# Another queue for the shift weights, earlier input transposes, and longer runs of the shift's sums

## The chip, the cores and the metric

The kernel runs on one core of one Trainium2 chip. The metric is the device time in microseconds (us). The kernel before has a median of 1969.03 us over 3 runs (1965.37 to 1971.18).

## The reference, cut to what matters

The program is one layer of an encoder over a prompt of 1024 tokens (width 2048) and 32 sample tokens, in float32. First the conditioning vector `c` of each of the two groups of tokens gives a shift, a scale and a gate by one matrix of 2048 x 6144. Then the input is normalised and modulated, and one wide projection gives the inputs of four branches:

```
shift, scale, gate = split(c @ w_mod + b_mod, 3)
u = layer_norm(x) * (1 + scale) + shift
(z_a, xbc_a, dt_a, q_b, k_b, v_b, g_b, ...) = split_cols(u @ w_in)
... four branches (state space, stick-breaking attention, mLSTM, convolution) ...
o = concat(y_a, y_b, y_c, y_d) @ w_out
x_new = layer_norm(ALPHA * x + (1 + gate) * o) * ln_g + ln_b
```

What the change touches is how `shift` and `scale` are computed at the start, and how the first `u` is made from `x`.

## The kernel before, in words

The prompt is done in two halves of 512 tokens; the 32 sample tokens ride with the first. `u` is kept transposed, as 16 tiles of 128 features by the tokens, and each tile is split into a high and a low part in a rounded float32 type (`uh`, `ul`), as are the weights (`wh`, `wl`). A product is three matmuls: `wh` by `uh`, `wh` by `ul`, `wl` by `uh` (lines 362 to 364, and 1437 to 1439 at the start). The shift is not added to `u`: it is two further columns of each tile (`shift_columns`, copied by GpSimd), so that the projection of the shift comes out of the same matmuls as two bias columns. A projection that takes those columns has to wait for the shift; one for the gates of branch B (`b_gate`, and the two gate tiles of `startup`) leaves them out and adds the bias later.

`startup` (line 1387) does what must come first. It loads and normalises the input (`load_norm`: five groups of rows, the last the 32 sample rows, four tiles of 512 columns each). It loads the scale's weights in four groups of 16 tiles of 256 KB (`quads`), and for each four tiles runs `mod_sum`: four float32 matmuls that write the four quarters of PSUM's partitions, called a quad here. When the 16 tiles of a group are summed, `mod_columns` copies the sum out of PSUM (VectorE), turns it by four transposes (TensorE), and adds and biases it into the scale of four feature tiles. Then `build_u0` makes these four feature tiles: four transposes of the input and one of the sample rows into PSUM, two scaling copies by ScalarE into `uf`, one rounding copy and one subtraction by VectorE, and a small subtraction by GpSimd. `part` multiplies four feature tiles by the weights of one gate tile, for one of two spans of tokens; four parts per group, two gate tiles by two spans. The order on TensorE and of the loads is written by hand here (`inorder`). In it, the parts of group g-1 stand between the transposes of group g.

After `startup` the rest is ordered by a planner. It simulates the program with costs of its own, puts each engine's instructions in the order in which that simulation finds them ready, and takes what the program lists first, or marks with `tc.high_priority()`, before the rest. Each engine then runs its list strictly in order. `weave` lists two more `b_gate` tiles together with the shift: `mod_group(g, 0)` for the four groups, 64 loads of 256 KB on SyncE's queue (SP), 16 quads, and four times `mod_columns`, which here ends in `shift_columns`. Then branch B's first unit follows: q, k and v of two heads, which need the shift columns.

Buffers: the pool `io` has 20 tiles, which hold the scale's and the shift's weights among others; `wk` has 13; `up` has 16 pairs for `uh` and `ul`, and 15 of the 20 input tiles are kept in it, the rest in `io`. PSUM's tags: `ip` 3 banks (accumulators of projections), `z` 2, `s` 2 and `a` 1. Nearly all loads go by SP's queue; GpSimd (POOL) issues only the stores of lines 1282 and 1340.

Of the kernel before, what the change touches and what calls it, by code (L numbers as in the profile page):

```python
# [6 lines left out]
F32 = mybir.dt.float32  # L7
# [55 lines left out]
def step_kernel(ctx, tc, xp, xs, cst, wmss, wmg, bgate, win, wsm, wout, lng, lnb, ck, cv,  # L63
# [136 lines left out]
    inorder = tc.keep_in_program_order  # L200
    begun = [None]

    def mod_sum(o, kq, ws):


        for i in (3, 0, 1, 2):
            c0 = 2 * (4 * kq + i)
            yield T.matmul(o[32 * i:32 * i + 32], cpad[:, c0:c0 + 32], ws[i][:, 0:512], start=(kq == 0),  # L208
                           stop=(kq == 3), skip_group_check=True)

    def mod_group(g, part):
        o = ZT("mod")
        for kq in range(4):
            ws = []
            for i in range(4):
                wr = IO("wmr")
                nc.sync.dma_start(wr[:, 0:512], wmss[g, 4 * kq + i, part])
                ws.append(wr)
                if i < 3:
                    yield 1  # L220
            with tc.high_priority():
                after = None
                for mm in mod_sum(o, kq, ws):
                    after = behind(mm, after)
# [26 lines left out]
    def load_norm(src, rows, keep):  # L251

        tiles = []
        for q in range(4):
            if keep and q < 3:
                t = up.tile([P, 546], F32, tag=("uh", "ul")[(len(keep) + q) % 2], name=nm("x"))
            else:
                t = (IO if keep else WK)("x")
# [12 lines left out]
        if keep:  # L271
            nb = SM(1, "bnb", 3)
            V.scalar_tensor_tensor(nb[:rows], mv[:rows, 0:1], -1.0, rs[:rows], op0=ALU.mult, op1=ALU.mult)
            for q in range(4):
                A.activation(tiles[q][:rows, 0:512], tiles[q][:rows, 0:512], AF.Identity, bias=nb[:rows],
                             scale=rs[:rows])
# [13 lines left out]
    def build_u0(xts, k):  # L290

        uh, ul = new_u(0, k)
        uf = WK("uf")
        q, o = divmod(k, 4)
        pt = ST("xt")
# [4 lines left out]
        for pp, n, c0, j in ((pt, 512, 0, 0), (pt2, SMP, 512, 1)):  # L300
            A.activation(uf[:, c0:c0 + n], pp[:, 0:n], AF.Copy, scale=scale1[:, k, j:j + 1])
        V.tensor_copy(uh[:, 2:546], uf[:, 0:544])
        return (G.tensor_tensor(ul[:, 514:546], uf[:, 512:544], uh[:, 514:546].bitcast(F32), op=ALU.subtract),
                V.tensor_tensor(ul[:, 2:514], uf[:, 0:512], uh[:, 2:514].bitcast(F32), op=ALU.subtract))
# [1081 lines left out]

    def startup():
# [27 lines left out]
        def quads(g):  # L1415
# [10 lines left out]
            for kq in range(4):  # L1426
                for mm in mod_sum(o, kq, ws[4 * kq:4 * kq + 4]):
# [18 lines left out]

        m = quads(0)
        for _ in range(3):  # L1450
            next(m)
        for g in range(4):
            o = next(m)
            m = quads(g + 1) if g < 3 else iter(())
            p = parts_of(g - 1) if g else iter(())
            next(p, None)
            mod_columns(g, 1, o, inorder)
            for i in range(4):
                if i < 3:
                    next(p, None)  # L1460
# [209 lines left out]
```

## Time and profile before

| | |
|---|---|
| Median of 3 runs | 1969.03 us |
| Profiled execution | 1967.32 us |
| Its span | 1965.3 us |
| TensorE busy | 1885.7 us, 96% |
| VectorE busy | 1343.0 us, 68% |
| ScalarE busy | 774.5 us, 39% |
| GpSimd busy | 320.5 us, 16% |
| Moved by DMA | 291.42 MB, mean 148 GB/s |

Times in the profile run from the start of the span. "Busy" is the time in which an engine had an instruction under way; matmuls overlap, so that two that start 0.127 us apart each show 0.29 us. In a row of the timeline, consecutive instructions of one kind are merged: its start, the time it takes as a whole, the engine, line, operation, tiles and shape, how many (x8), and, in brackets, how long the engine idled before it and what released it. A float32 matmul shows as two instructions, so that a quad is x8. PEclk is the clock granted to TensorE as a share of full speed.

### The profile page before, as it was taken

How to read it: one execution, taken by the hardware profiler on the slowest of the kernel's cores; microseconds unless marked ns; L12 is line 12 of the kernel's file. 1: busy time of each engine (PE TensorE's matmuls, PEld its weight loads, DVE VectorE, ACT ScalarE, POOL GpSimd, SP SyncE). 2: the span in 40 equal slices, each digit the busy share in tenths (PEclk: the TensorE clock that was granted, in tenths of full speed). 3: DMA queues.
4: the chain of work that ended last, by engine and by line, in shares of the span. 5: the costliest groups of instructions: out<-in, count | busy, mean ns of one | idle time of the engine just before them, and what ended most of it. 6: DMA issues, size and time to landing. Idle time of an engine off the chain costs nothing. (4 is left out here: it accounts for less than half of the span.)

```text
span 1965.3 us, 31995 instructions
## 1 busy us (share of the span) xinstructions
PE 1885.7 (96%) x12162; PEld 1570.6 (80%) x12162; DVE 1343.0 (68%) x2581; ACT 774.5 (39%) x1288; POOL 320.5 (16%) x542
## 2 busy tenths in 40 slices
PE   4999999999999999999999999999999899999997
PEld 1779899998888999976788786777878676778887
DVE  5416566967866858887778869885857673356665
ACT  5213433334564334545444444533335521133321
POOL 1100111211222202441101011121112320001000
PEclk9999999999999999999999999999999999999999
DMA  9885344334443343644232332432333654467643
GB/s 346 301 305 184 102 138 131 108 123 123 142 158 123 110 126 105 166 135 133 98 104 96 116 112 78 125 110 96 129 98 113 199 153 156 135 211 259 222 134 126
DMA packets 159930, 291.42 MB, mean 148 GB/s; under 512 B 23904, under 2 KB 66144, under 8 KB 159776
## 3 DMA queue, kind: packets, MB, share of 16 engines
q1 hardware_dynamic: 156960, 280.47, 44.5%
q0 software_dynamic: 2816, 8.92, 1.2%
q8 instruction: 95, 1.56, 0.3%
q14 instruction: 59, 0.48, 0.1%
HBM read 253.50 MB, written 35.82 MB: 147 GB/s over the span
## 5 line engine op out<-in xcount | busy, mean ns | idle before, releaser
L362 PE MATMUL ip<-uh,wh 128*128 128x512 f32 (+3 forms) x2304 | 759.0, 330 | 0.9 <-POOL uh L287 0.9
L364 PE MATMUL ip<-uh,wl 128*128 128x512 f32 (+3 forms) x2304 | 745.3, 323 | 0.0
L363 PE MATMUL ip<-ul,wh 128*128 128x512 f32 (+3 forms) x2304 | 745.1, 323 | 0.1
L337 ACT CAST wh<-wr 128x1024 fp32r<-128x1024 f32 x253 | 263.9, 1044 | 624.4 <-PE ip L363 343.1
L338 DVE TENSOR_TENSOR wl<-wr,wh 128x1024 fp32r<-128x1024 f32 x253 | 313.1, 1238 | 251.3 <-ACT wh L337 222.8
L362 PEld LDWEIGHTS ip<-uh,wh 128*128 128x128 f32 x2304 | 438.9, 191 | 45.2 <-issue 14.6
L364 PEld LDWEIGHTS ip<-uh,wl 128*128 128x128 f32 x2304 | 438.1, 190 | 31.7 <-issue 1.3
L363 PEld LDWEIGHTS ip<-ul,wh 128*128 128x128 f32 x2304 | 438.6, 190 | 30.9 <-issue 2.2
L1263 PE MATMUL op<-wh,yl 128*128 128x512 f32 (+1 forms) x576 | 215.2, 374 | 0.0
L1261 PE MATMUL op<-wh,yh 128*128 128x512 f32 (+1 forms) x576 | 214.9, 373 | 0.0
L1262 PE MATMUL op<-wl,yh 128*128 128x512 f32 (+1 forms) x576 | 214.4, 372 | 0.0
L1117 DVE SCALAR_TENSOR_TENSOR cv<-cin,cs,cv 128x574 f32<-128x574 f32 (+1 forms) x240 | 187.1, 780 | 2.6
L1263 PEld LDWEIGHTS op<-wh,yl 128*128 128x128 f32 x576 | 108.5, 188 | 25.6 <-issue 6.4
L1262 PEld LDWEIGHTS op<-wl,yh 128*128 128x128 f32 x576 | 108.5, 188 | 24.1 <-issue 4.8
L1261 PEld LDWEIGHTS op<-wh,yh 128*128 128x128 f32 x576 | 108.5, 188 | 22.7 <-issue 3.1
L809 POOL TENSOR_SCALAR_AFFINE_SELECT s<-s 128x128 f32<-128x128 f32 x64 | 38.3, 599 | 416.1 <-ACT s L708 415.8
L1170 DVE SCALAR_TENSOR_TENSOR gacc<-wg,cs,gacc 128x512 f32<-128x512 f32 x120 | 92.3, 789 | 11.0 <-DMA wg<-in_wmg_dram 10.9
L208 PE MATMUL mod<-wmr,cpad 128*32 128x512 f32 x256 | 38.4, 676 | 27.4 <-DMA wmr<-in_wmss_dram 27.2
L717 DVE TENSOR_TENSOR_SCAN pr<-kp 128x128 f32<-128x128 f32 (+4 forms) x66 | 53.7, 814 | 13.0 <-POOL kp L811 10.3
L721 DVE TENSOR_TENSOR s<-s,pr 128x512 f32<-128x512 f32 (+5 forms) x106 | 59.7, 566 | 1.8
L708 ACT ACTIVATE s<-z 128x512 f32<-128x512 f32 (+3 forms) x96 | 47.6, 496 | 33.1 <-PE z L738 30.5
L1071 POOL TENSOR_TENSOR dn<-dn,mhalf 128x1 f32<-128x1 f32 (+1 forms) x36 | 27.7, 770 | 194.3 <-DVE dn L1070 190.6
(384 smaller groups left out, 2342.1 us busy)
## 6 DMA issues: line engine op xcount, KB each, us to landing
wr<-in_win_dram SPq DMA_DIRECT2D x192, 512.0 KB
wmr<-in_wmss_dram SPq DMA_DIRECT2D x128, 256.0 KB
wr<-in_wout_dram SPq DMA_DIRECT2D x63, 512.0 KB
wg<-in_wmg_dram SPq DMA_DIRECT2D x64, 256.0 KB
x<-in_xp_dram SPq DMA_DIRECT2D x32, 256.0 KB
xr<-in_xp_dram SPq DMA_DIRECT2D x28, 256.0 KB
yf<-ysc SPq DMA_DIRECT2D x16, 272.0 KB
xk<-in_xp_dram SPq DMA_DIRECT2D x16, 256.0 KB
```

The costliest lines, as they stand in the source:

```text
L337: A.copy(wh, wr)
L338: V.tensor_tensor(wl, wr, wh.bitcast(F32), op=ALU.subtract)
L362: T.matmul(pt[:, 0:n], wh[:, k % 8, :], uh[:, c0:c0 + n], start=(k == 0), stop=False)
L363: T.matmul(pt[:, 0:n], wh[:, k % 8, :], ul[:, c0:c0 + n], start=False, stop=False)
L364: T.matmul(pt[:, 0:n], wl[:, k % 8, :], uh[:, c0:c0 + n], start=False, stop=(k == KD - 1))
L717: V.tensor_tensor_scan(pr[0:rows, 0:nk][:, ::-1], kp[0:rows, 0:nk][:, ::-1], kp[0:rows, 0:nk][:, ::-1], initial=init, op0=ALU.mult, op1=AL ...
L721: V.tensor_tensor(s[0:rows, 0:m], s[0:rows, 0:m], pr[0:rows, 1:m + 1], op=ALU.mult)
L1117: V.scalar_tensor_tensor(acc[:, 0:n], t[:, i:i + n], C("cdw", 31 * j + i), acc[:, 0:n], op0=ALU.mult, op1=ALU.add)
L1170: V.scalar_tensor_tensor(acc[j][:, 0:512], wr[:, 0:512], cT[:, k, j:j + 1], acc[j][:, 0:512], op0=ALU.mult, op1=ALU.add)
L1261: T.matmul(acc[t][:, 0:w], yh[:, c], wh, start=(first and i == 0), stop=False)
L1262: T.matmul(acc[t][:, 0:w], yh[:, c], wl, start=False, stop=False)
L1263: T.matmul(acc[t][:, 0:w], yl[:, c], wh, start=False, stop=(last and i == len(ws) - 1))
```

## The change

- The 64 loads of the shift's weights are issued by GpSimd on its own queue in place of SP's. During `startup` each of them is put behind one GpSimd instruction on GpSimd's list (`hold`: the small subtraction of feature tile 11).
- Twelve steps of the shift (12 loads and the first sum) are listed inside `startup`, ahead of the scale's last group.
- The shift's sums take eight weight tiles at once, as two quads in a row, in place of four. Group 0's accumulator is in PSUM tag `s`.
- `build_u0` is split. `turn_x` transposes the input of a feature tile and copies it, unscaled, from PSUM to SBUF (`xT`, mostly in free `up` tiles; ScalarE for odd tiles, VectorE for even ones). The new `build_u0` scales from SBUF: ScalarE writes `uh`, VectorE computes `x * scale - uh` in one instruction, and the 32 sample columns go by ScalarE and two GpSimd instructions.
- The transposes no longer wait for the scale. Two feature tiles are turned after each of the first three quads of group 0, and five in each of the loops of groups 0 and 1.
- The parts of group g now run in the loop of group g, between the quads of group g+1, with `mod_columns(g + 1)` ahead of the last part.
- In `load_norm`, VectorE normalises the odd ones of the four tiles, and the fourth tile is in `wk` in place of `io`.

```diff
-    def mod_sum(o, kq, ws):
+    def mod_sum(o, kq, ws, first, last):
     ...
     def mod_group(g, part):
-        o = ZT("mod")
-        for kq in range(4):
+        o = ST("mod") if g == 0 else ZT("mod")
+        for kq in range(0, 4, 2):
             ws = []
-            for i in range(4):
+            for i in range(8):
                 wr = IO("wmr")
-                nc.sync.dma_start(wr[:, 0:512], wmss[g, 4 * kq + i, part])
+                behind(nc.gpsimd.dma_start(wr[:, 0:512], wmss[g, 4 * kq + i, part]), hold[0])
                 ws.append(wr)
-                if i < 3:
+                if i < 7:
                     yield 1
             with tc.high_priority():
                 after = None
-                for mm in mod_sum(o, kq, ws):
-                    after = behind(mm, after)
+                for q in (1, 0):
+                    for mm in mod_sum(o, kq + q, ws[4 * q:4 * q + 4], kq == 0 and q == 1, kq == 2 and q == 0):
+                        after = behind(mm, after)
             yield 1
     ...
     def load_norm(src, rows, keep):
-                t = (IO if keep else WK)("x")
+                t = WK("x")
     ...
             for q in range(4):
-                A.activation(tiles[q][:rows, 0:512], tiles[q][:rows, 0:512], AF.Identity, bias=nb[:rows],
-                             scale=rs[:rows])
+                x = tiles[q][:rows, 0:512]
+                if q % 2:
+                    V.tensor_scalar(x, x, rs[:rows], nb[:rows], op0=ALU.mult, op1=ALU.add)
+                else:
+                    A.activation(x, x, AF.Identity, bias=nb[:rows], scale=rs[:rows])
     ...
-    def build_u0(xts, k):
-        uh, ul = new_u(0, k)
-        uf = WK("uf")
+    def turn_x(xts, k):
         q, o = divmod(k, 4)
+        xT = up.tile([P, 546], F32, tag=("uh", "ul")[k % 2], name=nm("xT")) if k < KD - 1 else IO("xT")
         pt = ST("xt")
         (four transposes into pt, one into pt2 = AT("xt2"), as before)
-        for pp, n, c0, j in ((pt, 512, 0, 0), (pt2, SMP, 512, 1)):
-            A.activation(uf[:, c0:c0 + n], pp[:, 0:n], AF.Copy, scale=scale1[:, k, j:j + 1])
-        V.tensor_copy(uh[:, 2:546], uf[:, 0:544])
-        return (G.tensor_tensor(ul[:, 514:546], uf[:, 512:544], uh[:, 514:546].bitcast(F32), op=ALU.subtract),
-                V.tensor_tensor(ul[:, 2:514], uf[:, 0:512], uh[:, 2:514].bitcast(F32), op=ALU.subtract))
+        if k % 2:
+            A.copy(xT[:, 0:512], pt)
+        else:
+            V.tensor_copy(xT[:, 0:512], pt)
+        V.tensor_copy(xT[:, 512:544], pt2[:, 0:SMP])
+        return xT
+
+    def build_u0(xT, k):
+        uh, ul = new_u(0, k)
+        x, h = xT[:, 0:512], uh[:, 2:514]
+        A.activation(h, x, AF.Copy, scale=scale1[:, k, 0:1])
+        x2, h2 = xT[:, 512:544], uh[:, 514:546]
+        A.activation(x2, x2, AF.Copy, scale=scale1[:, k, 1:2])
+        G.tensor_copy(h2, x2)
+        return (V.scalar_tensor_tensor(ul[:, 2:514], x, scale1[:, k, 0:1], h.bitcast(F32), op0=ALU.mult, op1=ALU.subtract),
+                G.tensor_tensor(ul[:, 514:546], x2, h2.bitcast(F32), op=ALU.subtract))
     ...
     def startup():
     ...
+        xT = []
+        def turn(n):
+            for _ in range(n):
+                xT.append(turn_x(xts, len(xT)))
         m = quads(0)
-        for _ in range(3):
-            next(m)
+        for n in (2, 2, 2, 0):
+            o = next(m)
+            turn(n)
+        mod_columns(0, 1, o, inorder)
         for g in range(4):
-            o = next(m)
+            for k in range(4 * g, 4 * g + 4):
+                begun[1:] = build_u0(xT[k], k)
+            if g == 2:
+                hold[0] = begun[2]
+                for _ in range(12):
+                    next(shift)
             m = quads(g + 1) if g < 3 else iter(())
-            p = parts_of(g - 1) if g else iter(())
-            next(p, None)
-            mod_columns(g, 1, o, inorder)
+            p = parts_of(g)
             for i in range(4):
-                if i < 3:
-                    next(p, None)
-                begun[1:] = build_u0(xts, 4 * g + i)
-                if i < 3:
-                    next(m, None)
-        for _ in parts_of(3):
-            pass
+                o = next(m, None)
+                if g < 2:
+                    turn(1)
+                if i != 2:
+                    next(p)
+            if g < 3:
+                mod_columns(g + 1, 1, o, inorder)
+            if g < 2:
+                turn(1)
+            next(p)
     ...
+    shift = chain(*[mod_group(g, 0) for g in range(4)])
     startup()
+    hold[0] = None
     ...
-            weave([(stage1(b_gate(p)), 2) for p in range(2, 4)], [(chain(*[mod_group(g, 0) for g in range(4)]), 64)])
+            weave([(stage1(b_gate(p)), 2) for p in range(2, 4)], [(shift, 52)])
```

## Rows read from the trace of the kernel before

**Rows 1.** The page, busy time by engine, and TensorE's in 40 slices.
```profile
PE 1885.7 (96%) x12162; PEld 1570.6 (80%) x12162; DVE 1343.0 (68%) x2581; ACT 774.5 (39%) x1288; POOL 320.5 (16%) x542
PE   4999999999999999999999999999999899999997
```

**Rows 2.** TensorE's waits in the span: engine, line, releaser, total us, times, longest.
```profile
PE mod L208 <- DMA wmr<-in_wmss_dram: 27.2, 11, 21.3
...
PE rt L495 <- DVE w L489: 4.4, 2, 2.5
...
PE ip L362 <- POOL uh L287: 0.9, 1, 0.9
```

**Rows 3.** Busy time by window: length, PE busy (count), PEclk, DMA share, GB/s.
```profile
21.26:94.00 72.74, 66.64 (x450) 1.00 0.94 334
94.00:155.00 61.00, 58.66 (x438) 1.00 0.87 306
```

**Rows 4.** TensorE's timeline, 21 to 39 us.
```profile
21.26 1.94 PE L208 MATMUL mod<-wmr,cpad 128*32 128x512 f32 x8 [21.26 <-DMA wmr<-in_wmss_dram]
24.16 1.94 PE L208 MATMUL mod<-wmr,cpad 128*32 128x512 f32 x8 [0.97 <-DMA wmr<-in_wmss_dram]
...
32.49 1.08 PE L233 MATMUL modc<-ident,mr 128*128 128x128 f32 x4 [0.98 <-DVE mr L231]
...
34.36 0.31 PE L299 MATMUL xt<-ident,x 32*128 32x32 f32 x1
...
36.70 1.11 PE L297 MATMUL xt<-ident,x 128*128 128x128 f32 x4
...
37.92 1.06 PE L208 MATMUL mod<-wmr,cpad 128*32 128x512 f32 x8
```

**Rows 5.** TensorE's timeline at 54.87 us, and at 93.80, the end of startup.
```profile
54.87 0.60 PE L297 MATMUL xt<-ident,x 128*128 128x128 f32 x4
55.40 0.24 PE L299 MATMUL xt<-ident,x 32*128 32x32 f32 x1
...
93.80 0.29 PE L362 MATMUL ip<-uh,wh 128*128 128x272 f32 x1
```

**Rows 6.** VectorE's and ScalarE's timelines before and after the first scale.
```profile
31.65 0.69 DVE L231 COPY mr<-mod 128x512 f32<-128x512 f32 x1 [5.96 <-PE mod L208]
33.84 0.17 DVE L240 SCALAR_TENSOR_TENSOR scale<-mods,cs 128x8 f32<-128x8 f32 x1
37.85 0.86 ACT L301 ACTIVATE uf<-xt,scale 128x512 f32<-128x512 f32 x2 [1.58 <-PE xt L297]
12.45 5.73 ACT L275 ACTIVATE x<-x,bnb,brs 128x512 f32<-128x512 f32 x8
```

**Rows 7.** VectorE on two SBUF inputs: duration ns min/median/max, first and last start.
```profile
L1170 DVE SCALAR_TENSOR_TENSOR gacc<-wg,cs,gacc x120: 655/744/1858, 456.8 to 1413.5; 128x512 f32<-128x512 f32 x120
L338 DVE TENSOR_TENSOR wl<-wr,wh x6: 1224/1224/1226, 94.1 to 141.1; 128x1024 fp32r<-128x1024 f32 x6
```

**Rows 8.** GpSimd's groups by line: count, busy us, mean ns, idle before.
```profile
L303 POOL TENSOR_TENSOR ul<-uf,uh 128x32 fp32r<-128x32 f32 x16 | 11.0, 684 | 72.4 <-DVE uh L302 72.4
```

**Rows 9.** TensorE's timeline around one quad (at 125.80) among projection matmuls.
```profile
125.58 0.29 PE L364 MATMUL ip<-uh,wl 128*128 128x272 f32 x1
...
127.03 0.28 PE L363 MATMUL ip<-ul,wh 128*128 128x272 f32 x1
```

**Rows 10.** TensorE's timeline at 149.75 us: half of a quad.
```profile
149.75 0.61 PE L208 MATMUL mod<-wmr,cpad 128*32 128x512 f32 x4
```

**Rows 11.** The shift's loads on SP, and one of SP's waits, 60 to 155 us.
```profile
L217 SPq DMA_DIRECT2D wmr<-in_wmss_dram x64: 327/382/1697, 68.7 to 143.7; - x64
SPq L333 <- DVE wl L338: 18.4, 7, 4.6
```

**Rows 12.** GpSimd's own DMA issues, line 1282: duration ns min/median/max; time to landing.
```profile
L1282 POOL DMA_DIRECT2D rsc<-val x20: 511/539/776, 1604.8 to 1775.0; - x20
DMA to landing us min/median/max: 2.3/4.4/7.9
```

More of the change, by code (lines that the diff above doesn't have):

```diff
@@ L200, in step_kernel @@
     inorder = tc.keep_in_program_order
+    hold = [None]
     begun = [None]
-    def mod_sum(o, kq, ws):
+    def mod_sum(o, kq, ws, first, last):
         for i in (3, 0, 1, 2):
             c0 = 2 * (4 * kq + i)
-            yield T.matmul(o[32 * i:32 * i + 32], cpad[:, c0:c0 + 32], ws[i][:, 0:512], start=(kq == 0),
-                           stop=(kq == 3), skip_group_check=True)
+            yield T.matmul(o[32 * i:32 * i + 32], cpad[:, c0:c0 + 32], ws[i][:, 0:512], start=first, stop=last, skip_group_check=True)
     def mod_group(g, part):
-        o = ZT("mod")
-        for kq in range(4):
+        o = ST("mod") if g == 0 else ZT("mod")
+        for kq in range(0, 4, 2):
             ws = []
-            for i in range(4):
+            for i in range(8):
                 wr = IO("wmr")
-                nc.sync.dma_start(wr[:, 0:512], wmss[g, 4 * kq + i, part])
+                behind(nc.gpsimd.dma_start(wr[:, 0:512], wmss[g, 4 * kq + i, part]), hold[0])
                 ws.append(wr)
-                if i < 3:
+                if i < 7:
                     yield 1
@@ L1384, in step_kernel, with chain @@
     rsc = dp.tile([5 * P, D], F32, name="rsc")
+    def chain(*gs):
+        for g in gs:
+            yield from g
     def startup():
@@ L1426, in quads @@
             for kq in range(4):
-                for mm in mod_sum(o, kq, ws[4 * kq:4 * kq + 4]):
+                for mm in mod_sum(o, kq, ws[4 * kq:4 * kq + 4], kq == 0, kq == 3):
                     inorder(mm)
@@ L1505, in stage1 @@
                 return
-    def chain(*gs):
-        for g in gs:
-            yield from g
     def stage_n(g, n):
```

## Prediction

> **What bounds the kernel now.** I read the busy shares first: TensorE is busy for 1885.7 of 1965.3 us, 96%, and in all but a few slices at nine tenths or more [rows 1]. So a microsecond of TensorE's work or idling that goes anywhere shortens the run by about that much, and time taken from other engines gives nothing. Next the waits of TensorE: of its idle time of some 80 us, 27.2 us are waits of the scale's and shift's quads for weights, 21.3 of them one wait, the first [rows 2]. By windows TensorE idles 72.74 - 66.64 = 6.1 us between its first quad and the end of startup, and 61.00 - 58.66 = 2.3 us in the stage of the shift [rows 3]. Last the timeline of the start. The first four quads wait for their loads, with idle times like the 0.97 us between them, and up to 37 us everything takes nearly twice as long as later: a quad 1.94 us against 1.06, four transposes 1.08 to 1.11 against 0.60 [rows 4, 5]. The granted clock reads 1.00 over the whole window [rows 3]; by the durations it is the lower of the two levels (1.2 GHz) until about 37 us and the higher (2.4 GHz) after. Before it rose TensorE had been at work from 32.49 to 37.9 us nearly without a gap, with transposes for more than half of that [rows 4].
>
> **Startup.** Before, it takes 93.80 - 21.26 = 72.5 us from the first quad to the first matmul behind it [rows 4, 5]. Of this, 6.1 us are idle. The lower clock costs 0.88 us for each of five quads (4.4), 0.48 for the first `mod_columns`, and about 0.5 for each of two groups of four transposes: 5.9 us. That leaves 60.5 us of work at the high clock, in which two of the shift's quads are included. The change adds and removes no TensorE instruction here; it orders them anew. So its startup ends at 21.26 + 60.5 + what the low clock costs + idle.
>
> The low clock: two feature tiles now follow each of the first three quads, so TensorE has no gap to wait in, and I charge the low level over a stretch as long as that from 32.49 to 37.9. In it a quad (0.88), two turned tiles (four transposes and one: 1.3 against 0.7, so 1.2 for both) and two thirds of the second quad (0.6) are slow: 2.7 us.
>
> Idle: the sample rows' transposes share one PSUM bank, and on VectorE a copy of 512 columns (0.69 [rows 6]) may stand ahead of the one that frees it: 0.3 for each of three pairs, 1.0. Ahead of the first scale, the copy of the sum and its handing on: 0.98 as before [rows 4]. From the end of the scale's transposes to the end of the first part: the scale itself 0.4 us (32.49 + 1.08 to 33.84 + 0.17), then per feature tile about 0.9 us of ScalarE (two activations took 0.86 [rows 6]), then VectorE's fused subtraction, which the start before does not have (line 1170, the same operation and size, took 0.74 [rows 7]), and three matmuls of 0.13: 0.4 + 4 x 0.9 + 1.2 + 0.4 of semaphores = 5.6 us. TensorE has one quad (1.1), one turned tile (0.7) and the part (1.55, twelve matmuls) to do meanwhile: 2.2 idle. The same chain stands ahead of groups 1 and 2 with a part, a quad and mostly a turned tile to cover it: 0 and 0.4. Ahead of group 3 only one part covers it: 2.8, of which the first eight-tile sum of the shift (2.1) fills most if its loads are there: 0.7. In all 1.0 + 1.0 + 2.2 + 0.4 + 0.7 = 5.3, and startup ends at 21.26 + 60.5 + 2.7 + 5.3 = 89.8 against 93.8: **4.0 us gained**. Bounds: 8.5 us (all of the low clock's 5.9 and half of the idle gone) and, if the low clock costs what it did and nothing fills the last chain, -1.3.
>
> The other engines' parts I cost at nothing. Ten of the 20 normalising steps go from ScalarE (5.73 / 8 = 0.72 us each [rows 6]) to VectorE, where they have no row: between nothing and the 0.74 of the fused operation [rows 7], so at most 7.4 us, beside loads that take until 21 us; I take 0.69, the copy of that size [rows 6]. GpSimd's added copy of 32 columns (its subtraction of 32 takes 0.68 [rows 8]; a plain copy no more, I take that) feeds only the second span's part, 1.55 us later; without that cover it would cost about 1 us per group.
>
> **The sums in pairs.** A quad among projection matmuls moves the next ones by 127.03 - 125.58 = 1.45 us, less two usual steps of 0.127: 1.20 us [rows 9]. The trace has no two quads in a row. The second costs at best what the second half of one does per four instructions, 1.06 - 0.61 = 0.45, so 0.90 [rows 4, 10], and at worst 1.20, no gain. I take 0.90, the nearer row, since only the weights change between them, as inside a quad: 8 pairs x 0.30 = **2.4 us gained** (0 to 2.4).
>
> **The shift's loads.** SP's list loses 64 issues that stood among the projections' weight loads, which sat 18.4 us on SP waiting for their buffers between 60 and 155 us, with shift loads queued behind them [rows 11]. On GpSimd 64 issues at 0.54 us [rows 12] are 35 us of an engine that is 16% busy [rows 1], and faster than the loads can move (262 KB at the 334 GB/s of the start: 0.78 us each [rows 3]). But on GpSimd they wait for `io` tiles, which only sums free, eight of 20 at a time, and `shift_columns` is queued behind them. And a sum, once it stands in TensorE's list, holds all that follows until its eighth load has landed. Of the 2.3 us idle here I count **1.6 us** as gained; bounds +2.3 and -14 (rival 1).
>
> The Trainium skill speaks against this edit: "SBUF — State Buffer", its section on the port that VectorE and GpSimd share, says that descriptors of DMAs issued by GpSimd are written by GpSimd, and that this is blocked while VectorE holds the shared port. The rows show GpSimd's issues at 0.51 to 0.78 us [rows 12], and in the shift's stage six splits of 1.22 us on VectorE [rows 7]. [...]
>
> **Sum.** 4.0 + 2.4 + 1.6 = 8.0 us. The profiled execution took 1967.3 us (span 1965.3 and 2.0 around it): 1959.3. The median of the runs is 1.7 above it, so by the median 1961.0; I forecast 1960.
>
> **Rivals.**
> 1. *TensorE stalls on the shift's sums: slower.* After the first 12 loads, 52 are left at about 80 us. TensorE can do without the last shift columns until about 140 us: it has 10 us of startup, 24.5 of two gate tiles (192 matmuls at 0.127), 14.7 of seven paired sums, 1.5 of columns, and about 10 of spans that leave the shift out, as far as three PSUM banks allow. So it decides at 60 / 52 = 1.15 us per load. For it: landings of 4.4 us in the median and up to 7.9 [rows 12], DMA engines already at 0.87 in that stage [rows 3], and eight waits in TensorE's order that the planner's costs may place too early. Against it: 0.54 us per issue. At 1.4 us per load the last columns are 13 us late and the 1.6 are not gained: 1959.3 + 13 + 1.6 = 1974.
> 2. *The clock stays low through the first pairs.* For it: before, four quads didn't raise it [rows 4], and the turned tiles wait for one PSUM bank between them. Against: it did rise after a stretch mostly of transposes [rows 4]. Then the first four quads and six turned tiles take 4 x 1.94 + 6 x 1.3 = 15.6 us and end at 36.9 in place of 33: 3.9 us lost, 1963.5 by the sum.
> 3. *The head start is not kept.* The next stage waits for other things: the narrow projection's chain on VectorE (4.4 us in two waits [rows 2]) and the loads of the second half's input, and the planner draws up TensorE's order there anew. Against: TensorE is at nine tenths nearly all the way [rows 1]. Half the gain goes: 1964.
> 4. *The early loads don't come early*, since 16 scale tiles and four weight tiles already fill the 20 of `io`: the last chain isn't filled: 2.1 us lost, 1962.
>
> **How the numbers follow.** Forecast 0.40, a fuller gain (1953: most of the low clock's cost and of the waits gone) 0.14, rival 1 0.16, rival 2 0.10, rival 3 0.13, rival 4 0.07. A measurement of this kernel can tell about 0.3%, 5.9 us, from no change. Faster: forecast, fuller gain and half of rival 4: 0.57. Slower: rival 1 and 0.01 of rival 3: 0.17. Same: the rest, 0.26. The range 1951 to 1970 takes in the fuller gain and the rivals but the worse half of rival 1; the forecast's own is 1956 to 1964.
>
> **What would show it.** In the trace after: six turned tiles before 33 us, and quads of 1.06 us from the third on; the first matmul after startup at 88 to 92 us; eight pairs of quads, each about 2.1 us; waits of the shift's sums under 1 us each; the last shift columns before 140 us. It is wrong if sums wait several microseconds for GpSimd's loads, if startup ends no earlier, or if TensorE's idle after 155 us grows by what the start gained.

## The result and the profile after

Predicted were 1960.0 us, 1951 to 1970. The changed kernel takes **1994.24 us** (median of 4 runs, 1990.24 to 1996.65), the kernel before 1970.11 beside it: a ratio of 1.0122, 95% interval 1.0094 to 1.0150. It is slower by some 24 us. The profiled execution took 1995.23 us, its span 1993.2.

Line numbers have moved: a quad of `mod` is L209 now, the shift's load L219, the scale's load L1441, POOL's subtraction L321, the first projection behind startup L379 (before: L362). The page of the changed kernel: busy time by engine, and TensorE's 40 slices.

```profile
PE 1894.4 (95%) x12162; PEld 1574.8 (79%) x12162; DVE 1349.3 (68%) x2599; ACT 772.5 (39%) x1286; POOL 355.6 (18%) x622
...
PE   5689999999999999999999999999999899999998
```

The number of TensorE's instructions is that of [rows 1]. In the slices the first three have changed, 4 9 9 to 5 6 8; all behind them is as it was but for the last digit. So the loss lies in the first 150 us. TensorE's timeline there, the changed kernel (start, duration, instructions, in brackets the idle time ahead and what ended it):

```profile
21.55 1.93 PE L209 MATMUL mod<-wmr,cpad 128*32 128x512 f32 x8 [21.55 <-DVE bst L268]
...
27.14 1.94 PE L209 MATMUL mod<-wmr,cpad 128*32 128x512 f32 x8
...
31.58 1.94 PE L209 MATMUL mod<-wmr,cpad 128*32 128x512 f32 x8
...
35.95 1.06 PE L209 MATMUL mod<-wmr,cpad 128*32 128x512 f32 x8
...
72.27 0.29 PE L1460 MATMUL ip<-uh,wl 128*128 128x272 f32 x1
85.47 3.64 PE L209 MATMUL mod<-wmr,cpad 128*32 128x512 f32 x16 [12.91 <-DMA wmr<-in_wmss_dram]
89.99 1.93 PE L209 MATMUL mod<-wmr,cpad 128*32 128x512 f32 x8 [0.88 <-DMA wmr<-in_wmss_dram]
...
99.31 1.07 PE L209 MATMUL mod<-wmr,cpad 128*32 128x512 f32 x8 [1.12 <-DMA wmr<-in_wmss_dram]
...
118.16 1.92 PE L209 MATMUL mod<-wmr,cpad 128*32 128x512 f32 x16 [2.28 <-DMA wmr<-in_wmss_dram]
...
121.14 0.29 PE L379 MATMUL ip<-uh,wh 128*128 128x272 f32 x1
```

The last row answers to 93.80 of [rows 5]: startup ends 27.3 us later. From the first quad to 72 us no wait is longer than 1.1 us. Then TensorE stands 12.91 us before the first sum of eight, which the change puts ahead of the scale's last group, and 0.88, 1.12 and 2.28 us more before later quads. The same stretches by windows (length, busy time and count of PE, PEld, DVE, ACT, POOL, granted clock, DMA share, GB/s), the changed kernel:

```profile
21.55:121.14 99.59, 76.62 (x449) 45.82 (x449) 36.10 (x77) 29.74 (x56) 26.63 (x58) 0.86 0.72 254
...
60.00:80.00 20.00, 12.31 (x89) 8.22 (x87) 6.54 (x15) 4.82 (x11) 7.65 (x18) 0.92 0.26 77
80.00:100.00 20.00, 12.53 (x72) 5.31 (x72) 0.00 (x0) 0.00 (x0) 2.92 (x6) 0.66 0.91 328
```

and the startup of the kernel before, cut at its own end:

```profile
21.26:93.80 72.54, 66.44 (x449) 40.16 (x450) 30.00 (x60) 29.01 (x54) 11.07 (x19) 1.00 0.94 334
```

Both rows hold 449 matmuls. TensorE idles 99.59 - 76.62 = 23.0 us against 6.1, which is 16.9 of the 27.05 us; the same matmuls take 76.62 us against 66.44, which is the other 10.2. Most of this second part is the clock: 0.66 granted from 80 to 100 us, behind the idle stretch, so partly at the lower level (1.2 GHz), and quads of 1.8 to 1.9 us again. Ahead of all this, from 60 to 80 us, the DMA engines moved 77 GB/s at a share of 0.26, in a stage that lives on its loads. POOL's and SP's timelines of the changed kernel say why:

```profile
75.57 0.24 POOL L321 TENSOR_TENSOR ul<-xT,uh 128x32 fp32r<-128x32 f32 x1
76.15 5.70 POOL L219 DMA_DIRECT2D wmr<-in_wmss_dram  x10 [0.34 <-issue]
82.20 1.20 POOL L219 DMA_DIRECT2D wmr<-in_wmss_dram  x2 [0.35 <-DMA wmr<-in_wmss_dram]
```

```profile
42.40 53.41 SPq L1441 DMA_DIRECT2D wmr<-in_wmss_dram  x32
```

The twelve early loads own their `io` tiles from the place where they are listed, but POOL issues them only at 76 us, behind its subtraction for k = 11. The scale's last sixteen loads on SP are listed behind them. Three of these go out at 67.4 to 68.6 us; the other thirteen need the tiles that the first sum of eight will free, and go out from 87.4 to 95.8 us. TensorE, SP and the DMA engines all wait for POOL: 3.6 us of the 12.91 pass before its first issue, the rest until the eight loads have landed.

### The profile page after: what moved, and what is told of

Same layout as the page of the kernel before. It is cut to its first block, busy times and chain, and to the rows that moved or that the text cites. A ratio compares the mean times of both kernels' runs of the same rounds, so it can differ in the third digit from the quotient of the medians.

```text
span 1993.2 us, 32081 instructions
## 1 busy us (share of the span) xinstructions
PE 1894.4 (95%) x12162; PEld 1574.8 (79%) x12162; DVE 1349.3 (68%) x2599; ACT 772.5 (39%) x1286; POOL 355.6 (18%) x622
## 5 line engine op out<-in xcount | busy, mean ns | idle before, releaser
L379 PE MATMUL ip<-uh,wh 128*128 128x512 f32 (+3 forms) x2304 | 757.5, 329 | 0.0
L379 PEld LDWEIGHTS ip<-uh,wh 128*128 128x128 f32 x2304 | 436.9, 190 | 37.3 <-issue 6.7
L826 POOL TENSOR_SCALAR_AFFINE_SELECT s<-s 128x128 f32<-128x128 f32 x64 | 36.9, 577 | 413.6 <-ACT s L725 413.3
L209 PE MATMUL mod<-wmr,cpad 128*32 128x512 f32 x256 | 38.2, 696 | 45.0 <-DMA wmr<-in_wmss_dram 23.5
```

The costliest lines, as they stand in the source:

```text
L379: T.matmul(pt[:, 0:n], wh[:, k % 8, :], uh[:, c0:c0 + n], start=(k == 0), stop=False)
```

## Experiments

Two readings go with each time; the kernel before took 1967.7 to 1970.1 us (medians) beside them. `ipn` is the narrow projection, the first tile of the next stage: when it starts tells how late startup and the shift's stage end. It starts at 174.9 us before and at 202.8 after, 27.9 later, the whole difference of the spans (1993.2 - 1965.3). The span behind it should not change between kernels, yet it was 1785.8 to 1797.0 us (before: 1790.4); so single spans and `ipn` differ by up to 7 us, and `ipn` is the better witness for this stage. Three profiles of one kernel (e6, e12, e16) put it at 174.8 to 176.9, so a difference of 2 us there tells nothing. The second reading is when the shift's loads were issued.

```
kernel                                   median  ratio [95%]               loads issued    ipn from
before                                                                     68.7 to 143.7     174.9
after                                   1994.24  1.0122 [1.0094, 1.0150]   76.2 to 159.2     202.8
e1  12 early, behind the scale's last   1972.73  1.0023 [1.0002, 1.0044]   74.9 to 135.1     178.9
e2  none early                          1978.07  1.0047 [1.0026, 1.0067]   86.0 to 149.8     186.5
e3  12 early, not held                  1987.48  1.0106 [1.0067, 1.0145]   56.7 to 154.4     197.9
e4  startup alone                       1970.59  1.0012 [0.9992, 1.0031]   71.8 to 148.2     179.1
e5  POOL's queue alone                  1983.49  1.0073 [1.0046, 1.0100]   85.9 to 149.9     187.8
e6  sums of eight alone                 1967.77  0.9985 [0.9965, 1.0005]   68.1 to 141.8     175.8
e7  4 early                             1983.48  1.0076 [1.0054, 1.0099]   70.7 to 142.9     189.0
e8  startup + POOL's queue              1984.65  1.0076 [1.0049, 1.0102]   83.6 to 146.6     186.3
e9  POOL's queue, POOL's work on DVE    1978.19  1.0058 [1.0024, 1.0092]   67.8 to 126.6     183.4
e10 startup + sums of eight             1973.45  1.0041 [1.0028, 1.0054]   71.7 to 147.6     179.4
e11 16 loads on SP, 48 on POOL          1970.57  1.0023 [1.0001, 1.0045]   69.7 to 137.0     181.1
e12 sums of eight alone, again          1965.06  0.9981 [0.9961, 1.0001]   68.4 to 142.7     174.8
e13 e10 with 56 loads                   1965.61  0.9991 [0.9979, 1.0004]   72.8 to 138.9     175.8
e14 e12 with 56 loads                   1963.52  0.9980 [0.9968, 0.9992]   69.3 to 134.8     173.0
e15 after, all loads on SP's queue      1974.29  1.0034 [1.0020, 1.0047]   56.3 to 142.6     177.8
e16 sums of eight alone, third time     1968.64  0.9996 [0.9980, 1.0012]   68.8 to 144.5     176.9
```

### The early loads: e1 to e4

The first theory (B) blamed the tiles. **e1** moves the early steps in `startup` behind the scale's last group, **e2** leaves them out, **e3** takes the hold away, **e4** keeps only the new startup (loads on SP's queue, sums of four).

```diff
 e1, in the loop of startup          e2: the "-" lines only; then weave (shift, 64)
-            if g == 2:
-                hold[0] = begun[2]
-                for _ in range(12):
-                    next(shift)
             m = quads(g + 1) if g < 3 else iter(())
...
+            if g == 2:
+                hold[0] = begun[2]
+                for _ in range(12):
+                    next(shift)
             next(p)
 e3
-                hold[0] = begun[2]
```

> The changed kernel with one thing moved: the twelve early steps of the shift are listed after the scale's last group has been listed, at the end of the loop of group 2, in place of ahead of it. Theory B (buffers): in the changed kernel the early shift loads are listed ahead of the scale's last 16 loads, so they are given io tiles first, but they cannot start until the small subtraction of feature tile 11 is done at 76 us; meanwhile the DMA engines idle and the first sum of eight holds TensorE 12.9 us. With the order turned, the scale's loads get the tiles: startup ends at 88 to 95 us, total 1960 to 1968. Rival Q (GpSimd's queue is slow): the sums still wait for loads, 1980 or more. Rival O (the new order of startup is slow by itself): startup still ends after 110 us, 1985 or more.

> The changed kernel without the twelve early steps: all 64 shift loads are listed after startup, still on GpSimd's queue, still in sums of eight. Theory B: startup ends at 89 to 93 us; the shift's sums wait a little longer at first, total 1963 to 1970. Rival Q: waits of the sums of 10 us or more in total after startup, 1978 or more. Rival O: startup ends after 110 us, 1985 or more.

> The changed kernel with the early shift loads where they are listed, but not put behind the subtraction of feature tile 11 on GpSimd. Theory B: the DMA engines no longer idle from 60 to 76 us, and the wait of 12.9 us ahead of the first sum falls below 4; the scale's last group still comes after 12 shift loads of 0.7 us, so startup ends at 95 to 105 us, total 1970 to 1982. Rival Q: the wait ahead of the first sum stays above 8 us, total 1988 or more. Rival O: 1985 or more.

> The changed kernel's startup (transposes spread, scaling from SBUF, parts in their own group's loop) with the shift as before: SP's queue, sums of four, all after startup. Theory B: startup ends at 88 to 93 us, the shift's stage as in the kernel before, total 1961 to 1968. Rival Q: the same, 1961 to 1968. Rival O: startup ends after 105 us, total 1980 or more.

Listed behind the scale's last group, the same early loads cost 4.0 us at `ipn` instead of 27.9: the place is worth 24 us. But no kernel came out below 1970, so the early loads were not all of it: e2, which has none, took 1978.1, as rival Q (POOL's queue) had it and theory B had not. e3 missed: the hold away, its first sum still waited 9.59 us and `ipn` was 23 us late, and POOL's timeline of e3 shows that the order on the queue held the loads all the same:

```profile
56.71 1.30 POOL L219 DMA_DIRECT2D wmr<-in_wmss_dram  x2 [0.36 <-DMA wmr<-in_wmss_dram]
67.52 0.21 POOL L319 CAST uh<-xT 128x32 fp32r<-128x32 f32 x1 [9.51 <-ACT xT L318]
68.04 0.54 POOL L219 DMA_DIRECT2D wmr<-in_wmss_dram  x1 [0.32 <-PE ip L1460]
```

Two loads went out at 56.7 us; the third stood behind POOL's cast of k = 8, which waited 9.51 us for ScalarE. e4 is no measurable change, 1.0012, though its startup looks shorter; to that below.

### One part at a time: e5 to e8

**e5** and **e6** are the kernel before with one part of the change, **e8** is e4 with POOL's queue, **e7** the changed kernel with 4 early steps for 12.

```diff
 e5 (on the kernel before), e8 (on e4)
-                nc.sync.dma_start(wr[:, 0:512], wmss[g, 4 * kq + i, part])
+                nc.gpsimd.dma_start(wr[:, 0:512], wmss[g, 4 * kq + i, part])
 e6: range(0, 4, 2), eight loads and two mod_sum calls per step, as in the change
 e7
-                for _ in range(12):
+                for _ in range(4):
```

> Kernel before with one edit: the shift's 64 loads are issued by POOL's queue, not SP's; sums stay at four, startup as before. Theory P (the queue itself costs: a load issued by POOL lands 5.4 us after its issue in the median in the changed kernel, and 538 ns are spent per issue): 1972 to 1977 us, the shift's waits on TensorE in 94 to 155 us grow by 3 us or more in all and its last quad comes after 152. Rival S (the sum of eight costs, since it sets eight tiles free at once instead of four): this run is within 2 us of the kernel before, last quad at 149 to 151.

> Kernel before with one edit: the shift's sums go over eight k tiles in a row, loads stay on SP's queue, startup as before. Theory P: within 2 us of the kernel before, 1966 to 1970, pairs of 1.9 to 2.1 us with waits under 1 us each. Rival S: 1972 to 1977, the waits ahead of the pairs at 1.5 us or more each and the last pair after 152 us.

> Changed kernel with the early steps at the same place, but only four of them in place of twelve: four loads, and no sum. Theory B (the early loads take tiles that the scale's last group needs, and the sum of eight stands ahead of that group's quads in TensorE's order): four tiles leave the last group its sixteen, so the wait of 12.91 us goes; the longest wait for a weight in 60 to 95 us is under 3 us, the first projection after startup comes at 90 to 97, and the time is 1972 to 1979, like the kernels with the early steps moved or left out. Rival H (early loads in POOL's queue behind k = 11's subtraction hurt by themselves, however few): a wait over 6 us stays, first projection after 105, 1984 us or more.

> Changed startup, and the shift's loads by POOL's queue after it, in sums of four; no early loads. With sums of eight (none early) it took 1978.1, with SP's queue and sums of four 1970.6. Theory P: 1975 to 1979, nearly all of those 7.5 us. Rival S: 1969 to 1973, the queue costs nothing and the sums of eight took them.

POOL's queue alone makes the kernel before slower by 0.73%, 14 us. With the changed startup, too (e4 to e8): 0.64% in time, 7.2 us at `ipn`. Sums of eight cost nothing (e6). e5 and e8 lost more than either theory expected of them; P had the sign, and the trace shows that its reason was wrong. POOL's timeline of e5, the end of startup:

```profile
85.21 0.75 POOL L303 TENSOR_TENSOR ul<-uf,uh 128x32 fp32r<-128x32 f32 x1 [0.38 <-DVE uh L302]
85.90 5.54 POOL L217 DMA_DIRECT2D wmr<-in_wmss_dram  x10
```

and all shift loads of e5 (duration ns min/median/max; first and last start):

```profile
L217 POOL DMA_DIRECT2D wmr<-in_wmss_dram x64: 538/538/731, 85.9 to 149.9; - x64
```

Once it has begun, POOL issues the 64 loads in 64.0 us; SP had taken 75.0 [rows 11]. The queue isn't slow. But POOL works in order, the last subtraction of startup stands ahead of its first load, and so that load leaves at 85.9 instead of 68.7 us. The program itself puts it there: what is listed behind startup goes behind startup's last instruction on the same engine (`begun`, lines 1470 and 1471), which cost nothing while POOL issued none of these loads. No run lifted this order alone. In those 17 us the DMA engines have little to do. The 20 us from 70 on by windows (columns as above), e5:

```profile
70.00:90.00 20.00, 19.38 (x141) 15.76 (x140) 10.48 (x22) 8.41 (x17) 8.03 (x14) 1.00 0.34 114
```

and the kernel before:

```profile
70.00:90.00 20.00, 19.61 (x145) 13.43 (x141) 10.37 (x21) 7.44 (x16) 4.09 (x9) 1.00 0.83 295
```

A share of 0.34 against 0.83 over 20 us is 9.8 us of transfer not done; `ipn` is 12.9 us late. TensorE's waits for these weights from 60 to 170 us (us in total, times, longest) show most of it, first e5, then the kernel before:

```profile
PE mod L208 <- DMA wmr<-in_wmss_dram: 9.9, 6, 4.5
...
PE mod L208 <- DMA wmr<-in_wmss_dram: 1.2, 3, 0.7
```

e7 missed both theories: the 12.9 us wait is gone, as B said, yet the kernel takes 1983.5. Its four early loads leave at 70.70 us, and the fifth behind the last of startup's subtractions:

```profile
70.70 2.52 POOL L219 DMA_DIRECT2D wmr<-in_wmss_dram  x4 [0.34 <-issue]
...
87.73 0.24 POOL L321 TENSOR_TENSOR ul<-xT,uh 128x32 fp32r<-128x32 f32 x1
88.24 5.39 POOL L219 DMA_DIRECT2D wmr<-in_wmss_dram  x10 [0.27 <-issue]
```

So e5, e7 and e8 lose the same thing: 12 to 17 us in which the stage's loads aren't issued (e8's first leaves 11.8 us behind e4's).

### Is it the queue's order? e9 to e12

```diff
 e9 (on e5): L287, L288 and L303
-        G.tensor_copy(uh[:, 0:2], shiftH[:, k, :].bitcast(F32))
+        V.tensor_copy(uh[:, 0:2], shiftH[:, k, :].bitcast(F32))
 ... and likewise for ul, and for startup's 128x32 subtraction
 e11 (on the kernel before)
-                nc.sync.dma_start(wr[:, 0:512], wmss[g, 4 * kq + i, part])
+                (nc.sync if g == 0 else nc.gpsimd).dma_start(wr[:, 0:512], wmss[g, 4 * kq + i, part])
 e10: e4 and e6 together.   e12: e6 once more
```

> Kernel before with the shift's loads on POOL's queue, as in the run that took 1983.5 us, and with POOL's own work of this stage given to VectorE: the sixteen 128x32 subtractions and the shift columns' copies. Theory I (a load on POOL's queue costs because POOL takes its work in order: the first of them stood behind the last subtraction of startup and was issued at 85.9 us, where SP issued it at 68.7): the first load is now issued at 68 to 74 us and the time is 1966 to 1974. Theory P (the queue itself is slow, 538 ns an issue and 5.6 us to landing): 1978 or more, wherever the first load stands.

> Kernel before; of the shift's 64 loads the first 16 (group 0) are issued by SP and the other 48 by POOL, with POOL's own work as before. Theory I: the first loads start at 68 to 69 us again and most of the 14 us is gone, 1967 to 1975 (a rest of 0 to 5 for loads that stand behind the shift columns' copies). Theory P: three quarters of the 14 us stay, 1977 to 1983.

> Changed startup and sums of eight, but the loads on SP's queue and none early: the change without POOL's queue. Theory I: 1966 to 1972, since the first shift load is issued at 71 to 73 us, 3 us later than before, and this stage ends with its loads; startup's head start does not reach the end. Theory P: the same. Rival W (the three parts need one another, sums of eight cost once startup is changed): 1976 or more, as with POOL's queue and no early loads (1978.1).

> Kernel before with sums of eight alone, loads on SP's queue, once more (1967.8, ratio 0.9985, 0.9965 to 1.0005, the first time): if the seven switches saved are worth what the kernel before shows for a quad that follows another (0.30 us less each, 2.4 in all), 1966 to 1968 and a ratio of 0.998 to 0.9995; if nothing of them reaches the end, a ratio within 0.9995 to 1.0005.

e11 is theory I's: with the first 16 loads on SP, behind the scale's, 10 of the 14 us are gone in the times and half of the 12.9 at `ipn`. Theory P would have kept three quarters.

```profile
L217 POOL DMA_DIRECT2D wmr<-in_wmss_dram x48: 538/538/731, 88.4 to 137.0; - x48
...
L217 SPq DMA_DIRECT2D wmr<-in_wmss_dram x16: 328/382/1284, 69.7 to 83.5; - x16
```

e9 missed theory I: it is slower by 0.58%, and its 1978.19 us are what theory P had. But P's reason, a slow queue, is not what the trace shows: the loads leave at 67.8 us as theory I had it and are all out at 126.6, 17 us before SP's in the kernel before. Nor is it POOL's work, now on VectorE: TensorE waits only 0.4 us more for that engine. TensorE's timeline of e9:

```profile
73.04 1.07 PE L208 MATMUL mod<-wmr,cpad 128*32 128x512 f32 x8 [1.45 <-DMA wmr<-in_wmss_dram]
...
79.23 1.24 PE L208 MATMUL mod<-wmr,cpad 128*32 128x512 f32 x8 [3.66 <-DMA wmr<-in_wmss_dram]
...
106.03 5.08 PE L208 MATMUL mod<-wmr,cpad 128*32 128x512 f32 x24 [4.13 <-ACT graw L750]
```

The scale's last two quads now wait 5.1 us for weights; before, they ran at 69.62 and 71.54 without a wait. SP issued those weights at 67.5 us at the latest, as before, but POOL's loads go out beside them from 67.8 on, where on SP's queue they would have gone behind. What each queue moved in e9 from 70 to 80 us (packets, MB, share of the engines), first POOL's, then SP's:

```profile
q0 software_dynamic: 694, 2.31, 61.1%
q1 hardware_dynamic: 580, 1.23, 36.5%
```

POOL's loads took the larger part; in the kernel before, SP's queue moved 3.65 MB in these 10 us. The Trainium skill, "DMA: Bandwidth & Descriptors", section "Issuing engines are not separate DMA queues", says that transfers started by several engines run on the same 16 DMA engines and interleave; this trace agrees, with those 2.31 and 1.23 MB side by side and the 5.1 us. The second loss, three sums in a row behind a wait of 4.13 us, is another order of TensorE's list; why the planner drew it up so I didn't try. So two things are shown of POOL's queue: behind POOL's work the loads come late, and free of it they take their share from loads that are wanted sooner.

### Startup's head start, and the early loads on SP: e13 to e16

The changed startup without POOL's queue (e10) was expected at 1966 to 1972 and took 1973.45. The two cut kernels leave out every eighth load:

```diff
 e13 (on e10), e14 (on e12)
-                wr = IO("wmr")
-                nc.sync.dma_start(wr[:, 0:512], wmss[g, 4 * kq + i, part])
+                if i < 7:
+                    wr = IO("wmr")
+                    nc.sync.dma_start(wr[:, 0:512], wmss[g, 4 * kq + i, part])
                 ws.append(wr)
 e15 (on the changed kernel)
-                behind(nc.gpsimd.dma_start(wr[:, 0:512], wmss[g, 4 * kq + i, part]), hold[0])
+                nc.sync.dma_start(wr[:, 0:512], wmss[g, 4 * kq + i, part])
 e16: e6 a third time, with more runs
```

> Changed startup, sums of eight, SP's queue, none early (1973.5), and of each eight tiles of the shift's weights only seven are loaded: the eighth product uses the seventh tile, so the shift computed is another, with the same products on TensorE and 2 MB less to load. Theory L (the stage after startup ends with its loads, whose first one is issued 3 us later than before): 2 MB at about 310 GB/s are 6.8 us, so 1966 to 1969. Rival N (the loss lies on TensorE or in startup itself): 1971.5 to 1974.

> Startup as before, sums of eight on SP's queue (1965 to 1968), and again 56 loads for 64, the eighth product from the seventh tile. Theory L: TensorE waits only 3 us for weights here, so this gains at most those, 1962 to 1966, clearly less than the same cut gains with the changed startup. Rival N: the cut is worth the same with both startups.

> Changed kernel with the shift's loads on SP's queue; the twelve early ones stand at the same place, ahead of the scale's last group, and nothing holds them. Theory B (place in the order: twelve of twenty tiles taken, and the shift's sum of eight ahead of the last group's quads on TensorE): the last group's loads stand behind the early ones, so a wait for weights of 3 to 8 us stays in 65 to 95 us and the time is 1974 to 1984, above the 1973.5 without early loads. Rival H (POOL's queue is needed for the loss): no wait over 2 us, 1966 to 1973.

> Kernel before with sums of eight alone, a third time, with more rounds. If the gain of 0.15 to 0.2% is real: a ratio of 0.997 to 0.9995 with an interval below 1. If not: an interval that holds 1 in its middle.

Eight loads fewer, with the same matmuls, are worth 0.50% with the changed startup (1.0041 to 0.9991) and 0.09% with the old one (from the mean of the three ratios of e6, e12 and e16, weighted by their intervals, 0.9989, to 0.9980). That is theory L's direction and, in the first case, 9.8 us where it had 6.8. At `ipn` the two are nearer: 3.6 us (179.4 to 175.8) against 2.8 (the mean of 175.8, 174.8 and 176.9, to 173.0). By windows from 92 us to `ipn`, first e10, then e13:

```profile
92.00:179.40 87.40, 81.85 (x635) 69.29 (x635) 29.66 (x66) 15.74 (x25) 5.71 (x34) 1.00 0.84 284
...
92.00:175.80 83.80, 81.80 (x640) 70.10 (x639) 31.91 (x75) 16.02 (x26) 6.60 (x34) 1.00 0.79 274
```

TensorE is busy as long in both, and its idle time falls from 5.6 to 2.0 us: all of the 3.6. So the loads share in setting the end of this stage with either startup; that they weigh more with the new one is shown by the times and hardly by the trace.

e15 is the clearest of all: the changed kernel, its order of tiles and sums untouched, only the queue given back, and with it the hold gone, which alone (e3) was worth little. It takes 1974.29 us, about as much as with no early loads at all (e10). SP's and TensorE's timelines of e15:

```profile
56.32 9.86 SPq L219 DMA_DIRECT2D wmr<-in_wmss_dram  x12
66.27 13.57 SPq L1441 DMA_DIRECT2D wmr<-in_wmss_dram  x16
...
80.88 9.85 SPq L219 DMA_DIRECT2D wmr<-in_wmss_dram  x11
```

```profile
70.90 1.92 PE L209 MATMUL mod<-wmr,cpad 128*32 128x512 f32 x16
74.62 1.06 PE L209 MATMUL mod<-wmr,cpad 128*32 128x512 f32 x8 [1.80 <-DMA wmr<-in_wmss_dram]
...
78.44 1.07 PE L209 MATMUL mod<-wmr,cpad 128*32 128x512 f32 x8 [1.03 <-DMA wmr<-in_wmss_dram]
...
83.82 1.06 PE L209 MATMUL mod<-wmr,cpad 128*32 128x512 f32 x8 [1.61 <-DMA wmr<-in_wmss_dram]
```

The twelve early loads go out at 56.3 to 66.2 us, the sum of eight runs at 70.9 us without a wait, and the scale's last group waits 1.80, 1.03 and 1.61 us. The order that theory B blamed costs these 4.4 us when its loads leave in turn; the wait and the time are what B expected, at the lower edge of both. On POOL's queue the same order costs 25 us more at `ipn` (202.8 against 177.8), and 20 us more in e3, which has no hold either, so that only the queue differs (197.9).

e16 leaves the sums of eight at no change that this kernel's measurement can tell.

## Why the prediction was wrong

**The shift's loads, the step that failed.** The prediction counted 1.6 us of gain for giving them to POOL. It compared POOL's 0.54 us per issue with the transfer's 0.78 and asked whether POOL keeps pace. It does: 538 ns in the median, 64 loads in 64 us (e5). It never priced what stands ahead of the first load. The prediction named what is queued *behind* POOL's loads (`shift_columns`), and not the sixteen subtractions *before* them, of which the last ran at 85.2 us, while SP was free for the first load at 68.7. Alone this edit costs 14 us in the time and 12.9 at `ipn`. Rival 1 had the sign and, with 13 us, nearly this size, for the wrong reason: it priced a slower pace, and the loss is a late start.

**The last chain of startup, the second half of the loss.** "The first eight-tile sum of the shift (2.1) fills most if its loads are there: 0.7." They weren't there: the early loads were issued at 76 us, in front of a sum that stood in TensorE's order at 72.5. The prediction knew that these loads wait for tiles; it didn't follow the tiles on to those listed behind, the scale's last sixteen, of which thirteen waited for the sum. Rival 4, at 2.1 us, saw the tiles full but took the early loads for the ones that would suffer. Measured: 16.9 us more of idle in startup, and 10.2 of longer matmuls, most of it at the lower clock behind the wait. On SP's queue the same order takes 4.4 us of waits (e15), behind the scale's loads 4.0 at `ipn` in all (e1).

**Startup, 4.0 us.** In e4, where nothing else is changed, it takes 92.10 - 22.24 = 69.86 us against 72.54, 2.7 less. But it holds less work. The shift's quads that run inside startup are four in the kernel before (the prediction counted two) and two in e4. The quads' rows by window (length, busy time and count of PE, of PEld, clock, DMA share, GB/s), first the kernel before, then e4:

```profile
21.26:93.80 72.54, 25.65 (x160) 3.36 (x160) 1.00 0.94 334
...
22.24:92.10 69.86, 20.71 (x144) 3.02 (x144) 1.00 0.90 323
```

and the stretch from there to `ipn`, all engines:

```profile
93.80:174.90 81.10, 78.76 (x595) 65.39 (x594) 29.40 (x66) 14.18 (x23) 4.76 (x34) 1.00 0.83 283
...
92.10:179.10 87.00, 80.96 (x610) 65.73 (x609) 29.45 (x66) 14.01 (x23) 5.71 (x34) 1.00 0.83 284
```

The two quads come later in e4 and make this stretch 80.96 - 78.76 = 2.2 us longer in work. So startup gained 2.7 - 2.2 = 0.5 us, not 4.0. Its idle came out as forecast (5.2 us against 5.3), and so did its clock (two quads and two turned tiles slow, about 3.0 us against 2.7). The term that failed here is the 60.5 us of work at the high clock, taken as unchanged by the new order: TensorE was busy for 64.7 us, with the two quads 66.9, less the 3.0 some 64. Why the same matmuls take that much longer in this order stays open.

Behind startup TensorE idles 6.0 us in e4 against 2.3, of which waits for the shift's weights are 4.0 against 1.2. In the new order projection matmuls run ahead of the last quads; the last of these come later (the scale's last two run from 75.35 to 77.3 us, where before the last ran at 71.54); their tiles come free later; and the shift's loads, which need the tiles, begin 3.1 us later and end 4.5 us later than before (the table; [rows 11]). `ipn` is then 4.2 us late: the first quad 1.0 later, 0.5 gained, 3.7 more idle. The prediction took TensorE for the bound since it is 96% busy, and let a head start on it pass on to the end. The stage of the shift ends with its loads as well, as e13 shows. There was little head start, and rival 3 was right that none would be kept, though for another reason than those it named.

**The clock, 2.7 us in this sum.** Rival 2 came true in the changed kernel: three quads at 1.93 to 1.94 us, the fourth at 35.95 at 1.06, four quads and six turned tiles done at 37.0 as rival 2 had it (36.9). In e4, with the same order, the third quad already ran at 1.06:

```profile
27.42 1.94 PE L209 MATMUL mod<-wmr,cpad 128*32 128x512 f32 x8
...
31.00 1.06 PE L209 MATMUL mod<-wmr,cpad 128*32 128x512 f32 x8
```

So the moment of the rise is not fixed by this order, and the charge was right in one run and 3 us short in the other.

**The sums in pairs, 2.4 us.** The size on TensorE was right. A pair in e12, among projection matmuls:

```profile
128.70 0.29 PE L363 MATMUL ip<-uh,wh 128*128 128x274 f32 x1
128.92 1.92 PE L208 MATMUL mod<-wmr,cpad 128*32 128x512 f32 x16
...
131.00 0.29 PE L365 MATMUL ip<-uh,wl 128*128 128x274 f32 x1
```

131.00 - 128.70 = 2.30, less two steps of 0.127, is 2.05 us, against twice 1.20 [rows 9]: 0.35 saved per pair where 0.30 were forecast. The whole is a ratio of 0.9989, 0.9978 to 0.9999 by the weights above: 2.2 us, under what a single comparison tells. And `ipn` does not start sooner (175.8, 174.8, 176.9 against 174.9), probably for the same reason, the loads; e14's 173.0 with fewer of them points that way.

**The rule on the shared port.** POOL's 64 issues in the changed kernel (duration ns min/median/max; first and last start):

```profile
L219 POOL DMA_DIRECT2D wmr<-in_wmss_dram x64: 538/538/743, 76.2 to 159.2; - x64
```

That is what [rows 12] had; they aren't lengthened, and the eight that overlap a split on VectorE took 538 ns each. The Trainium skill, "SBUF — State Buffer", section "SBUF: two separate sides", has GpSimd's descriptors blocked while VectorE runs an operation in a mode that takes both ports; by the page's section "Who interferes with whom", a subtraction of two SBUF inputs, as the splits are, has no such mode and did not stall a DMA. This trace agrees, with those 538 ns; a stall of the first kind no run here shows. That page's advice, to issue such loads from another queue, would have been right here on other grounds.

**What would have shown it.** Six turned tiles before 33 us: 36.0. First matmul behind startup at 88 to 92: 121.1, and 92.1 in e4 with two quads fewer ahead of it. Waits under 1 us: 12.91, 2.28 and others. The last shift columns before 140: 169.3. Only the pairs held.

**What stays open.** The parts don't add up: e10 to e2 adds POOL's queue for 7.1 us at `ipn` but only 0.06% in the time, and e10's own 0.41% is nearly twice what its 4.5 us at `ipn` make. The stages behind `ipn` move by some microseconds from kernel to kernel, and no run here told why. The other PSUM tag for group 0's sum, which e2 has and e10 has not, was not tried alone. No kernel that does all the work was faster than the one before by a margin that counts; its startup and its queue stay.

## What to carry to other kernels

When a DMA is moved to another engine's queue, write down what stands ahead of it there and when that is done; the first issue matters before the pace does. An engine that computes late in a stage is the wrong one to start the next stage's loads, however idle it is on average. When two versions of a stage are timed, count the instructions in both first: e4's startup was shorter mainly because two quads had left it. And where buffers circulate, a load listed early owns its buffer from then on: if it can't be issued at once, all that is listed behind it waits for an engine that has nothing to do with it.

## What was not expected of the hardware

POOL issued loads at a steady 538 ns and finished 64 of them sooner than SP did (64.0 us against 75.0), though a load took 5.6 us in the median to land in e5. The granted clock fell to 0.50 in the stretch from 80 to 90 us, behind 12.91 us in which TensorE only waited, and startup's 449 matmuls took 10.2 us longer than before, most of it behind that wait: such a stall cost this kernel a good deal more than its own length.
